# A two-block model on one core: block 2's modulation products on ScalarE and GpSimd instead of VectorE

## Chip, cores and metric

One Trainium2 chip, one NeuronCore of it. The metric is the device time of one execution in microseconds (us); a lower number is better.

## The reference, cut to what matters

Two transformer-like blocks are applied to `x` of shape 1 x 256 x 2048 (256 tokens, 2048 channels), all in float32. Each block derives six vectors of 2048 numbers from a conditioning vector `c` and uses them to shift, scale and gate the channels:

```python
c_act = jax.nn.silu(c_2)
ada = (c_act @ w_ada + b_ada)[:, None, :]        # w_ada: 2048 x 12288
sh1, sc1, gt1, sh2, sc2, gt2 = jnp.split(ada, 6, axis=-1)
h = _rms(x, g_norm1) * (1 + sc1) + sh1
...
x = x + gt1 * (merged @ w_out)
h2 = _rms(x, g_norm2) * (1 + sc2) + sh2
gate, up = jnp.split(h2 @ w_ffn_in, 2, axis=-1)
x = x + gt2 * ((jax.nn.silu(gate) * up) @ w_ffn_out)
```

That is block 2; block 1 has a recurrent mixer instead of attention and modulates in the same way. The change touches `c_act @ w_ada` of block 2: a product of a vector with a matrix of 2048 x 12288, 100.7 MB of weights that are read once.

## The kernel before

The tokens' activations stay on the chip (`xT`, channels on the 128 partitions). All weights stream from memory once, in loads of 128 x 2048 float32 (1 MB) into tiles called `raw`. Four `raw` tiles rotate (`rawp`), a fifth (`rawx`) joins during the two feed-forward parts; every load, of whatever weight, takes the next tile in turn, and all loads are issued in one fixed order on the SyncE queue.

**Matrix products.** A weight in `raw` is split into a high half `H` (ScalarE, line 333) and a low half `L` (VectorE, line 334: `raw` minus `H`, both read from SBUF), in pieces of 128 x 1024, four tiles of each. TensorE multiplies with both (lines 412 and 414 in the wide form): one load of weights is two pieces, and 16 pairs of matmuls. At the end of a strip of 512 outputs the PSUM tiles are taken over by a ScalarE copy and a VectorE add (`take`, lines 444 and 445), or added to `xT` by VectorE (line 747).

**Modulation products.** `gemv` (line 209) computes 1024 of the outputs of `c_act @ w_ada` without TensorE's matmuls: each load of `w_ada` holds two rows-of-128 by 1024 columns, and for each of the two, VectorE multiplies by the channel's silu(c) (a column of `cact`, one number per partition) and adds into the accumulator `acc` in one instruction (line 230; the first of the 16 products only multiplies, line 228). At the end TensorE transposes `acc` in eight pieces of 128 x 128 (line 241), VectorE sums over the partitions' former axis (line 242) and adds the bias (line 243). There are two accumulators (`accp`).

In block 2 this is done twelve times (six vectors, two halves): 12 x 16 = 192 products of 128 x 1024, of which 180 add and 12 only multiply. `Background` mixes them into the matrix products: after each load of a matrix product it runs as many steps as are due, and one step is one `w_ada` load with its two products. Three groups are started: `ada_a` (SC1, SH1, GT1; 6 x 16 = 96 products, one step per load, line 903) while the second half of block 1's feed-forward part runs; `ada_b` (SC2, SH2; 64 products, a step every 1.8 loads, line 1246) during attention; `ada_c` (GT2; 32 products, a step every 3 loads, line 1343) in block 2's feed-forward part. In the trace `ada_a` fills the stretch from 754 to 1089 us, called stage A below; `ada_b` the one from some 1370 to 1735 us, stage B; and `ada_c` one that ends at 2060 us.

The tile framework's scheduler then fixes the order of each engine's instructions when the program is built. Each engine runs its own list in order; semaphores make it wait.

Of the kernel before, what the change touches and what calls it, by code (L numbers as in the profile page):

```python
# [11 lines left out]
AF = mybir.ActivationFunctionType  # L12
ALU = mybir.AluOpType
# [67 lines left out]
def kernel(ctx: ExitStack, tc: tile.TileContext, a: dict, out: bass.AP):  # L81
    nc = tc.nc
    V, S, TE = nc.vector, nc.scalar, nc.tensor
# [13 lines left out]
    def ax_tile():  # L97
        return pax.tile([P, 512], F32, tag="ax", name="ax")
# [97 lines left out]
    def raw_tile(whole_only=False):  # L196
        if whole_only and spare:
            pool_, tag = spare[0]
            spare.append(spare.pop(0))
            return pool_.tile([P, 2048], F32, tag=tag, name="raw")  # L200
        turn_[0] = (turn_[0] + 1) % (4 + len(extra))
        if turn_[0] >= 4:
            pool_, tag = extra[turn_[0] - 4]
            return pool_.tile([P, 2048], F32, tag=tag, name="raw")
        return rawp.tile([P, 2048], F32, tag="raw", name="raw")
# [3 lines left out]
    def gemv(blk, parts, k0=0, nk=8):  # L209

        w = a["w_ada_2" if blk else "w_ada"][0]
        width = nk * P
        per = 2048 // width
        accs = [accp.tile([P, 1024], F32, tag="acc", name="acc") for _ in parts]
        for kt in range(0, KD, per):
            raws = []
            for part in parts:
                raw = raw_tile()
                rv = raw[:, :per * width].rearrange("p (k n) -> p k n", n=width)
                c0 = part * D + k0 * P  # L220
                nc.sync.dma_start(out=rv, in_=w[kt * P:(kt + per) * P, c0:c0 + width].rearrange("(k p) n -> p k n", p=P))
                raws.append(rv)
            for k in range(per):
                cc = cact[:, blk, kt + k:kt + k + 1]
                for acc, rv in zip(accs, raws):
                    av = acc[:, :width]
                    if kt + k == 0:
                        V.tensor_scalar(av, rv[:, k, :], cc, None, ALU.mult)
                    else:
                        V.scalar_tensor_tensor(av, rv[:, k, :], cc, av, ALU.mult, ALU.add)  # L230
                if len(parts) == 2 and k == per // 2 - 1:
                    yield
            yield
        for part, acc in zip(parts, accs):
            b = col["b_ada_2" if blk else "b_ada"][:, part * KD + k0:part * KD + k0 + nk]
            red = tiny.tile([P, nk], F32, tag=f"red{nk}", name="red")
            for q in range(0, nk, 4):
                n = min(4, nk - q)
                pt = ax_tile()
                for j in range(n):  # L240
                    TE.transpose(pt[:, j * P:(j + 1) * P], acc[:, (q + j) * P:(q + j + 1) * P], ident)  # L241
                V.tensor_reduce(red[:, q:q + n], pt[:, :n * P].rearrange("p (j t) -> p j t", t=P), AX.X, ALU.add)
            V.tensor_tensor(mods[:, blk, part, k0:k0 + nk], red, b, ALU.add)
            made.update((blk, part, k) for k in range(k0, k0 + nk))
            yield

    def whole(blk, part):
        return chain(gemv(blk, (part,), 0), gemv(blk, (part,), 8))
# [410 lines left out]
    def ada_group(i_sc, i_sh, k0, nk, paired=False):  # L659
        return gemv(0, (i_sc, i_sh), k0, nk) if paired else chain(gemv(0, (i_sc,), k0, nk), gemv(0, (i_sh,), k0, nk))  # L660
# [238 lines left out]
    def phase(half):  # L899
        if half == 0:  # L900
            bg.add(chain(*[gemv(0, (GT2,), k, 4) for k in range(0, KD, 4)]), 1.0, f"mods0{GT2}")
        else:
            bg.add(chain(whole(1, SC1), whole(1, SH1), whole(1, GT1)), 1.0, "ada_a")
# [492 lines left out]
```

## Time and profile before

| | us |
|---|---|
| median of 3 runs | 2543.78 |
| lowest, highest run | 2538.77, 2544.87 |
| the profiled execution, its own time | 2539.71 |
| its span, first to last instruction | 2538.0 |

| engine | busy us | share of the span |
|---|---|---|
| TensorE (PE), matmuls | 2451.8 | 97% |
| VectorE (DVE) | 1907.2 | 75% |
| ScalarE (ACT) | 1175.9 | 46% |
| GpSimd (POOL) | 12.1 | 0% |
| DMA, mean over the span | | 71% |

The profile comes from one execution and names its instructions by engine, line and tile: `L<-raw,H` is an instruction that writes `L` from `raw` and `H`. A group's row gives how often it ran, how long all of it was busy and one on average, and how long its engine had stood idle before it and for whom. PEld is TensorE's loading of weights into the array, and overlaps with PE. SPq is SyncE's queue, which issues the loads.

### The profile page before, as it was taken

The numbers are of one execution on the slowest core, as the hardware profiler recorded it, in microseconds if no ns is written. First come the engines' busy times: TensorE is split into PE (matmuls) and PEld (weight loads), VectorE is DVE, ScalarE is ACT, GpSimd is POOL, SyncE is SP. The second block draws the span as 40 slices with busy tenths as digits, with TensorE's granted clock in tenths as the row PEclk, the third lists the DMA queues.
The fourth block names the chain that finished last, engine by engine and source line by source line (L and its number), as shares of the span: only waits on it lengthen the run. The fifth ranks groups of instructions, "written<-read, shape, count | busy, mean of one in ns | idle before, by whom it ended". The sixth has DMA issues, their size and how long they took to land.

```text
span 2538.0 us, 36716 instructions
## 1 busy us (share of the span) xinstructions
PE 2451.8 (97%) x14677; PEld 2170.6 (86%) x14677; DVE 1907.2 (75%) x2593; ACT 1175.9 (46%) x1620; POOL 12.1 (0%) x87
## 2 busy tenths in 40 slices
PE   4989989999999999999999999999999999999999
PEld 3678989999888888888888888888788888888888
DVE  7789978977988989968757678796866665555554
ACT  2146235345334444446655447744544443444443
POOL 1000000000000000000000000000000000000000
PEclk7999989999999999999999999999999999999999
DMA  9988978966989998846547776676576765555552
GB/s 332 360 297 293 357 256 297 331 201 223 324 309 328 336 351 314 315 141 196 181 132 259 275 279 232 232 271 243 193 247 232 251 221 183 187 195 183 187 196 99
DMA packets 287548, 637.05 MB, mean 251 GB/s; under 512 B 13328, under 2 KB 18832, under 8 KB 287120
## 3 DMA queue, kind: packets, MB, share of 16 engines
q1 hardware_dynamic: 287376, 634.69, 71.4%
q8 instruction: 115, 1.88, 0.3%
q14 instruction: 57, 0.47, 0.1%
HBM read 632.56 MB, written 2.10 MB: 250 GB/s over the span
## 4 chain that ended last, share of the span: by engine, by line
PE 90%; DVE 6%; ACT 2%; DMA 2%; issue 1%; SPq 0%; ACTq 0%; DVEq 0%
PE mm L412 42%; PE mm L414 22%; PE mm L425 5%; PE mm L423 4%; PE mm L424 4%; PE mm L420 3%; DVE acc L230 2%; PE mm L477 2%; PE mm L478 2%; PE mm L476 2%; DVE L L334 1%; PE ax L241 1%; ACT H L333 1%; DMA raw<-in_w_out_dram 1%; PE mm L466 1%
## 5 line engine op out<-in xcount | busy, mean ns | idle before, releaser
L334 DVE TENSOR_TENSOR L<-raw,H 128x1024 fp32r<-128x1024 f32 (+2 forms) x816 | 954.0, 1178 | 416.2 <-ACT H L333 408.5
L333 ACT ACTIVATE H<-raw 128x1024 fp32r<-128x1024 f32 (+2 forms) x816 | 828.4, 1023 | 902.9 <-PE mm L412 631.5
L412 PE MATMUL mm<-hH,H 128*128 128x512 f32 x1536 | 546.6, 396 | 2.0 <-DVE hH L345 1.7
L412 PE MATMUL mm<-hL,H 128*128 128x512 f32 x1536 | 544.6, 395 | 0.0
L230 DVE SCALAR_TENSOR_TENSOR acc<-raw,cact,acc 128x1024 f32<-128x1024 f32 (+2 forms) x450 | 479.8, 1068 | 26.9 <-DMA raw<-in_w_ada_dram 20.8
L412 PE MATMUL mm<-fhl,H 128*128 128x512 f32 x1408 | 494.7, 395 | 0.6 <-ACT H L333 0.5
L414 PE MATMUL mm<-hH,L 128*128 128x256 f32 x1536 | 433.8, 283 | 2.1 <-DVE L L334 2.0
L414 PE MATMUL mm<-hL,L 128*128 128x256 f32 x1536 | 433.3, 283 | 0.0
L414 PE MATMUL mm<-fhl,L 128*128 128x256 f32 x1408 | 395.3, 284 | 4.6 <-DVE L L334 4.4
L412 PEld LDWEIGHTS mm<-hH,H 128*128 128x128 f32 x1536 | 289.3, 189 | 70.8 <-issue 3.7
L412 PEld LDWEIGHTS mm<-hL,H 128*128 128x128 f32 x1536 | 288.2, 188 | 66.8 <-issue 1.3
L412 PEld LDWEIGHTS mm<-fhl,H 128*128 128x128 f32 x1408 | 264.3, 188 | 61.0 <-ACT H L333 1.2
L414 PEld LDWEIGHTS mm<-hH,L 128*128 128x128 f32 x1536 | 289.5, 189 | 3.3 <-DVE L L334 2.9
L414 PEld LDWEIGHTS mm<-hL,L 128*128 128x128 f32 x1536 | 288.8, 188 | 0.5
L414 PEld LDWEIGHTS mm<-fhl,L 128*128 128x128 f32 x1408 | 264.3, 189 | 6.9 <-DVE L L334 6.4
L423 PE MATMUL mm<-hH,H 128*128 128x256 f32 x512 | 146.0, 286 | 4.9 <-ACT H L333 3.3
L425 PE MATMUL mm<-hH,L 128*128 128x256 f32 x512 | 145.7, 285 | 0.8 <-DVE L L334 0.8
L424 PE MATMUL mm<-hH,H 128*128 128x256 f32 x512 | 145.5, 284 | 0.0
L423 PE MATMUL mm<-hL,H 128*128 128x256 f32 x512 | 144.1, 282 | 0.8 <-ACT H L333 0.8
L425 PE MATMUL mm<-hL,L 128*128 128x256 f32 x512 | 143.9, 282 | 0.4 <-DVE L L334 0.3
L424 PE MATMUL mm<-hL,H 128*128 128x256 f32 x512 | 143.9, 281 | 0.0
L423 PEld LDWEIGHTS mm<-hH,H 128*128 128x128 f32 x512 | 98.0, 192 | 5.9 <-ACT H L333 3.5
(353 smaller groups left out, 2709.1 us busy)
## 6 DMA issues: line engine op xcount, KB each, us to landing
raw<-in_w_ada_dram SPq DMA_DIRECT2D x168, 1024.0 KB, 6.4
raw<-in_w_ffn_in_dram SPq DMA_DIRECT2D x88, 1024.0 KB, 4.8
raw<-in_w_in_dram SPq DMA_DIRECT2D x84, 1024.0 KB, 5.2
raw<-in_w_ffn_down_dram SPq DMA_DIRECT2D x44, 1024.0 KB, 7.2
raw<-in_w_ffn_out_dram SPq DMA_DIRECT2D x44, 1024.0 KB, 5.1
raw<-in_w_out_dram SPq DMA_DIRECT2D x32, 1024.0 KB, 6.3
raw<-in_w_ffn_gate_dram SPq DMA_DIRECT2D x26, 1024.0 KB, 7.1
raw<-in_w_ffn_up_dram SPq DMA_DIRECT2D x26, 1024.0 KB, 6.8
```

The costliest lines, as they stand in the source:

```text
L230: V.scalar_tensor_tensor(av, rv[:, k, :], cc, av, ALU.mult, ALU.add)
L333: S.activation(dh, src, AF.Copy)
L334: V.tensor_tensor(dl, src, dh.bitcast(F32), ALU.subtract)
L412: TE.matmul(o, wh[:, sl], both.rearrange("p i t -> p (i t)"), start=i == 0, stop=False, skip_group_check=True)
L414: TE.matmul(o[:, 0:T], wl[:, sl], both[:, 0, :], start=False, stop=i == n_k - 1, skip_group_check=True)
L420: TE.matmul(o, wh[:, sl], act(k0 + k), start=first, stop=last, skip_group_check=True)
L423: TE.matmul(o, wh[:, sl], both[:, 0, :], start=first, stop=False, skip_group_check=True)
L424: TE.matmul(o, wh[:, sl], both[:, 1, :], start=False, stop=False, skip_group_check=True)
L425: TE.matmul(o, wl[:, sl], both[:, 0, :], start=False, stop=last, skip_group_check=True)
L476: TE.matmul(o, xh[:, ts], wh[:, cs], start=first, stop=False)
L477: TE.matmul(o, xh[:, ts], wl[:, cs], start=False, stop=False)
L478: TE.matmul(o, xl[:, ts], wh[:, cs], start=False, stop=last)
```

## The change

For block 2 (`blk` is 1) each product becomes two instructions: ScalarE multiplies the piece of `raw` by silu(c) in place, and GpSimd adds it into the accumulator. The first product of each accumulator is a single ScalarE instruction that writes `acc`. Block 1 keeps the old form.

```diff
@@ -224,7 +224,12 @@
                 cc = cact[:, blk, kt + k:kt + k + 1]
                 for acc, rv in zip(accs, raws):
                     av = acc[:, :width]
-                    if kt + k == 0:
+                    if blk and kt + k == 0:
+                        S.activation(av, rv[:, k, :], AF.Copy, scale=cc)
+                    elif blk:
+                        S.activation(rv[:, k, :], rv[:, k, :], AF.Copy, scale=cc)
+                        nc.gpsimd.tensor_tensor(av, av, rv[:, k, :], ALU.add)
+                    elif kt + k == 0:
                         V.tensor_scalar(av, rv[:, k, :], cc, None, ALU.mult)
                     else:
                         V.scalar_tensor_tensor(av, rv[:, k, :], cc, av, ALU.mult, ALU.add)
```

Every later line of the file stands five lower in the changed kernel: the split at 333 and 334 is at 338 and 339 there, the wide matmuls at 417 and 419, the transposes at 246.

**Stage A, VectorE before and ScalarE now.** This is the end of stage A's last strip of gate and up products and the start of its down products. On VectorE before (`f`, `fhl` are the feed-forward part's hidden values):

```order
L230 SCALAR_TENSOR_TENSOR acc<-raw,cact,acc 128x1024
L845 TENSOR_TENSOR f<-f,g 128x512
L230 SCALAR_TENSOR_TENSOR acc<-raw,cact,acc 128x1024
L334 TENSOR_TENSOR fhl<-f,fhl 128x2x256
L334 TENSOR_TENSOR L<-raw,H 128x1024 x2
L230 SCALAR_TENSOR_TENSOR acc<-raw,cact,acc 128x1024 x2
```

On ScalarE in the changed kernel, at the same place:

```order
L449 ACTIVATE f<-mm 128x256
L338 ACTIVATE fhl<-f 128x2x256
L338 ACTIVATE H<-raw 128x1024
L230 ACTIVATE raw<-raw,cact 128x1024 x2
L338 ACTIVATE fhl<-f 128x2x256
L338 ACTIVATE H<-raw 128x1024 x2
L230 ACTIVATE raw<-raw,cact 128x1024 x2
```

The pair of products per load has left VectorE's list, where it stood between the pairs of `L` splits, and its multiplications now stand between ScalarE's pairs of `H` splits. The additions are two rows of 90 on GpSimd's list, which holds little else from there on.

**Stage A, SyncE's queue.** Five loads in stage A's second strip of gate weights; `DMAHW` is the semaphore of an earlier load, the other one says whose work on the tile's former content must be over. Before:

```order
L371 DMA raw<-in_w_ffn_gate_dram 128x4x512 [waits DMAHW5_49,DVE_49]
L371 DMA raw<-in_w_ffn_gate_dram 128x4x512 [waits DMAHW4_49,DVE_49]
L221 DMA raw<-in_w_ada_dram 128x2x1024 [waits DMAHW6_49,DVE_49]
L371 DMA raw<-in_w_ffn_gate_dram 128x4x512 [waits DMAHW0_49,DVE_49]
L221 DMA raw<-in_w_ada_dram 128x2x1024 [waits DMAHW7_49,DVE_49]
```

Now:

```order
L376 DMA raw<-in_w_ffn_gate_dram 128x4x512 [waits DMAHW5_49,Pool_49]
L376 DMA raw<-in_w_ffn_gate_dram 128x4x512 [waits DMAHW4_49,DVE_49]
L221 DMA raw<-in_w_ada_dram 128x2x1024 [waits DMAHW6_49,Pool_49]
L376 DMA raw<-in_w_ffn_gate_dram 128x4x512 [waits DMAHW0_49,Pool_49]
L221 DMA raw<-in_w_ada_dram 128x2x1024 [waits DMAHW7_49,DVE_49]
```

A load into a tile that held `w_ada` weights waits for GpSimd's second addition now, and all loads behind it on the queue wait with it. The loads' order is the old one but for two places in the whole program: one `w_ada` load stands a row earlier, and one, in stage B, seven loads later.

**Stage A, TensorE, the last transposes.** `ax` is the PSUM tile that the transposes of `acc` write; the rows are those around the last end of `ada_a`, with the semaphores that each waits for. Before:

```order
L412 MATMUL mm<-fhl,H 128x512
L414 MATMUL mm<-fhl,L 128x256
L241 MATMUL ax<-ident,acc 128x128 x8
L412 MATMUL mm<-fhl,H 128x512 [waits Activation_49]
L414 MATMUL mm<-fhl,L 128x256 [waits DVE_49]
```

Now:

```order
L419 MATMUL mm<-fhl,L 128x256
L246 MATMUL ax<-ident,acc 128x128 [waits Pool_49]
L246 MATMUL ax<-ident,acc 128x128 x3
L417 MATMUL mm<-fhl,H 128x512 [waits Activation_49]
L417 MATMUL mm<-fhl,H 128x512 x3
L246 MATMUL ax<-ident,acc 128x128 x2
L419 MATMUL mm<-fhl,L 128x256 [waits DVE_49]
```

The transposes wait for GpSimd now, and the first of them stands 32 matmuls earlier in TensorE's list than before. At the other eleven ends the first of them stands at its old place, and the wait is for GpSimd there too.

## Rows read from the trace of the kernel before

**Rows 1.** The page: busy time of each engine, share, instructions.

```profile
PE 2451.8 (97%) x14677; PEld 2170.6 (86%) x14677; DVE 1907.2 (75%) x2593; ACT 1175.9 (46%) x1620; POOL 12.1 (0%) x87
```

**Rows 2.** Busy time by stretch; columns as the first row names them.

```profile
core 0: us, PE busy (x) PEld busy (x) DVE busy (x) ACT busy (x) POOL busy (x), PEclk, DMA share, GB/s
754.00:1089.00 335.00, 329.77 (x1879) 287.14 (x1878) 295.10 (x327) 149.13 (x191) 0.00 (x0) 0.99 0.90 330
...
1390.00:1735.00 345.00, 341.84 (x1903) 296.45 (x1902) 279.75 (x362) 196.36 (x258) 0.00 (x0) 1.00 0.76 264
```

**Rows 3.** The same stretches, only instructions on `acc`: PE, weight loads, DVE, clock, DMA.

```profile
754.00:1089.00 335.00, 6.50 (x47) 5.55 (x48) 119.74 (x96) 0.99 0.90 330
...
1390.00:1735.00 345.00, 4.14 (x32) 3.67 (x32) 69.51 (x56) 1.00 0.76 264
```

**Rows 4.** DVE groups from 754 to 1089 us: count, busy, mean ns, idle before.

```profile
L334 DVE TENSOR_TENSOR L<-raw,H 128x1024 fp32r<-128x1024 f32 x115 | 138.2, 1220 | 18.9 <-ACT H L333 18.3
L230 DVE SCALAR_TENSOR_TENSOR acc<-raw,cact,acc 128x1024 f32<-128x1024 f32 x90 | 115.3, 1281 | 1.5 <-DMA raw<-in_w_ada_dram 0.6
...
L334 DVE TENSOR_TENSOR fhl<-f,fhl 128x512 fp32r<-128x512 f32 x10 | 6.9, 687 | 0.2
L845 DVE TENSOR_TENSOR f<-f,g 128x512 f32<-128x512 f32 x10 | 6.8, 684 | 0.0
...
L880 DVE TENSOR_TENSOR ssg<-ssg,sq 128x256 f32<-128x256 f32 x7 | 2.9, 418 | 0.0
```

**Rows 5.** What TensorE waited for, 754 to 1089 us: total us, times, longest.

```profile
PE mm L414 <- DVE L L334: 4.4, 2, 2.7
```

**Rows 6.** The same from 1089 us to the end.

```profile
PE ax L318 <- DVE diag L316: 6.5, 2, 3.6
PE mm L414 <- DVE L L334: 2.7, 2, 2.0
```

**Rows 7.** ACT groups from 754 to 1089 us.

```profile
L333 ACT ACTIVATE H<-raw 128x1024 fp32r<-128x1024 f32 x115 | 119.7, 1056 | 130.3 <-PE mm L412 92.3 <-DMA raw<-in_w_ffn_down_dram 17.5 <-PE mm L414 6.2
...
L879 ACT ACTIVATE sq<-xT,cols 128x256 f32<-128x256 f32 x7 | 3.6, 507 | 6.0 <-DVE xT L747 6.0
L879 ACT ACTIVATE sq<-xT 128x256 f32<-128x256 f32 x7 | 2.8, 401 | 0.0
```

**Rows 8.** POOL groups of the whole span.

```profile
L574 POOL TENSOR_SCALAR_AFFINE_SELECT bands<-bands 128x256 f32<-128x256 f32 x4 | 1.6, 396 | 0.0
...
L574 POOL TENSOR_SCALAR_AFFINE_SELECT bands<-bands 128x128 f32<-128x128 f32 x4 | 1.2, 290 | 0.0
```

**Rows 9.** DVE line L578: duration ns min/median/max; first and last start us.

```profile
L578 DVE TENSOR_TENSOR bands<-bands,ident x8: 278/288/375, 7.5 to 14.6; 128x128 f32<-128x128 f32 x8
```

**Rows 10.** Timeline around 7.5 us, POOL and DVE: start us, us, instruction.

```profile
7.36 0.40 POOL L576 TENSOR_SCALAR_AFFINE_SELECT bands<-bands 128x256 f32<-128x256 f32 x1
...
7.52 0.38 DVE L578 TENSOR_TENSOR bands<-bands,ident 128x128 f32<-128x128 f32 x1
...
7.71 0.34 POOL L576 TENSOR_SCALAR_AFFINE_SELECT bands<-bands 128x128 f32<-128x128 f32 x1
```

**Rows 11.** Timeline of two ends: last two products, then transposes.

```profile
1019.30 2.60 DVE L230 SCALAR_TENSOR_TENSOR acc<-raw,cact,acc 128x1024 f32<-128x1024 f32 x2
...
1024.74 0.49 PE L241 MATMUL ax<-ident,acc 128*128 128x128 f32 x3
...
1076.32 2.60 DVE L230 SCALAR_TENSOR_TENSOR acc<-raw,cact,acc 128x1024 f32<-128x1024 f32 x2
...
1088.33 1.04 PE L241 MATMUL ax<-ident,acc 128*128 128x128 f32 x8
```

**Rows 12.** What load issues on SP waited for, 754 to 1089 us.

```profile
SPq L371 <- DVE acc L230: 63.4, 28, 4.9
...
SPq L221 <- DVE acc L230: 31.2, 14, 6.4
```

**Rows 13.** Busy time of VectorE line L334 alone by stretch.

```profile
1390.00:1735.00 345.00, 147.05 (x127) 1.00 0.76 264
```

## The prediction

> **What bounds the kernel now.** The page's first part comes first: TensorE is busy for 97% of the span, VectorE for 75%, ScalarE for 46%, and GpSimd has next to nothing to do [rows 1]. A share over the whole span says little about one stage, so the next view is busy time by stretch [rows 2]. The work of the change lies in three stretches; the same view for instructions on `acc` alone counts the products: 96 of the 192 run in stage A, within 335 us, and 56 of the other 96 within the 345 us of stage B [rows 3]. Stage A is where things are dense: TensorE 329.8 of 335 us, VectorE 295.1 (88%), ScalarE 149.1 (45%), transfers 90% [rows 2]. VectorE does two kinds of work there in about equal parts, 115 `L` splits (138 us) and 96 products (120 us) [rows 3, 4]. That looks like an engine worth relieving. But the question is what TensorE waits for, and the view of its waits answers: in stage A, 4.4 us in all for VectorE's `L` [rows 5]; after it to the end, 2.7 us for `L`, and 6.5 us in the norms' short chains, where no product is queued [rows 6]. So the kernel is bound by TensorE. VectorE, at 88%, is the next in line and almost never late.
>
> **The change part by part.** The sum starts at the profiled execution's own 2539.7 us; the median of the three runs, 2543.8, lies 4.1 above, and I add that at the end. About 0.3% (7.6 us) is the least that a measurement of this kernel can tell from no change.
>
> *What leaves VectorE:* 180 multiply-adds of 1.281 us and 12 multiplications of some 0.75 us, 240 us in all, of which 120 in stage A [rows 3, 4]. The gain is bounded by what TensorE waits for behind them: nothing at the least, 4.4 + 2.7 = 7.1 us at the most [rows 5, 6]. I take 2.7, the part outside stage A, because inside stage A the last term below takes VectorE's new room away again.
>
> *What ScalarE gets:* 192 multiplications. A 128x1024 copy takes 1.056 us; a scale read from a column costs 0.106 us more (the same square with and without it: 0.507 and 0.401) [rows 7]. That is 1.16 us each, 223 us in all, and 96 x 1.16 = 111 us in stage A, where ScalarE goes from 149 to 260 of 335 us (78%). The cover is its idle time: in stage A it stood 92 us before its splits because TensorE had not yet freed an `H` tile [rows 7]. A multiplication can stand before a PSUM take-over or a split for 1.16 us, as a product of 1.28 us stood before VectorE's half of the same work. I cost it at nothing. Without that cover, each of stage A's 13 strip ends could lose 1.16 us, 15 us in all.
>
> *What GpSimd gets:* 180 additions of 128x1024 with both inputs in SBUF, 90 in stage A. The trace has no such row. GpSimd's nearest ones read one input: 128x128 in 0.290 us and 128x256 in 0.396 [rows 8], so 0.83 ns per element and 0.18 us fixed. That gives three prices: 1.03 us if the second input costs nothing, 1.88 if each input costs what the one does, 2.73 if the write costs as much again. I take 1.88, since the row's one price already holds a write. Stage A's additions then take 90 x 1.88 = 169 us, half of the stage. In a pure count GpSimd keeps up easily.
>
> *What the additions wait for, and who waits for them.* Before, the two products of a load ended 2.6 us after their start; now it is 1.16 + 2 x 1.88 = 4.9 us, 2.4 later. Behind it are two waits. First, the `raw` tile is freed later: 28 loads of matrix weights in stage A had their issue held by a product, 63.4 us together, and 14 `w_ada` loads, 31.2 us [rows 12]; each is now 2.4 us later. The `H` and `L` tiles, split two loads ahead, cover that: ScalarE waited more for TensorE (92.3 us) than for the down weights' transfers (17.5) [rows 7]. If that cover went, 28 x 2.4 = 67 us would show. Second, the transposes of `acc` in TensorE's list wait for the last addition. The last product ended at 1019.30 + 2.60 = 1021.9 and the transposes began at 1024.74; at the last end 1078.9 and 1088.33, where they now stand 32 matmuls earlier, 32 x 335/1879 = 5.7 us, so the room of 9.4 shrinks to 3.7 [rows 2, 11]. Both hold 2.4 us. I cost them at nothing.
>
> *What the two engines cost each other.* This is the term that decides. In the first microseconds VectorE runs eight equal subtractions of two SBUF inputs, beside GpSimd's mask building. Their median is 0.288 us, the longest 0.375 [rows 9], and a long one, at 7.52, lies beside a GpSimd instruction that reads SBUF; the GpSimd instruction next to it took 0.34 us where 0.290 is usual [rows 8, 10]. So VectorE with two SBUF inputs and a reading GpSimd slow each other down, both of them. The Trainium skill (SBUF — State Buffer, "Who interferes with whom") says that such a pair shares an exclusive lock and that the later one fully blocks until the other is done; the row above agrees with its sign, and by the rule the sum is the one that I take, while by the row's 0.09 us alone nothing would be lost. If they take turns, their times add up. VectorE's instructions with two SBUF inputs in stage A are the splits (138.2 + 6.9), `f` times `g` (6.8) and the two sums of squares (2 x 2.9), 157.7 us [rows 4]; with GpSimd's 169 that is 327 of 335 us. Two in-order engines do not fill a stage to 98%: the fullest one behind TensorE filled 88% of it. At that filling 327 us need 327 / 0.881 = 371 us, 36 more than the stage has, and TensorE waits for `L` in that time. In stage B, 60 additions take 113 us beside 147 us of splits [rows 13], 260 / 0.881 = 295 of 345 us: nothing there, nor in the last stretch.
>
> The sum is 2539.7 - 2.7 + 36 = 2573 us, and with the 4.1 us to the median **2577 us**, slower by 1.3%. The Trainium skill (GPSIMD Engine Reference, section 3.1) gives 4497 ns for an addition of 2048 elements, from which I estimate 2.25 us here; the same sum would be 2616 us by that.
>
> **The rivals.**
>
> *Hidden.* The turn-taking costs only some 0.09 us per VectorE instruction whatever its size, as the one row shows. 115 x 0.09 = 10 us of VectorE's time vanish in the 160 us that it has spare once the products are gone. For it: TensorE's waits are tiny now. Against it: 0.09 us is most of what a 128-element instruction spends on its data, so nothing says that it stays 0.09 at 1024. Time 2544 (2540 to 2550).
>
> *Faster.* VectorE's room shows: the `L` splits in the down products of stage A no longer queue behind products, and all of TensorE's waits for `L` go, 7.1 us, with 0.5 us or so of small ones around them. It decides in this direction only if a split beside an addition loses less than its share of the room, some 1 us. Time 2536. Against it: it needs nearly every wait to go, and none to come.
>
> *Heavier.* An addition costs more than 1.88 us; halfway to the upper price, 2.3, stage A needs (207 + 158) / 0.881 = 414 us, 79 more: 2620. At 2.73 it would be 458 and 2664. For it: nothing in the trace shows a two-input instruction on GpSimd.
>
> *The transposes.* GpSimd falls behind by two loads, 4 x 1.88 = 7.5 us, and TensorE stands at the ends of `ada_a` before transposes whose last addition is 7.5 + 2.4 = 9.9 us late against rooms of 2.8 and 3.7 us [rows 11]: 7.1 + 6.2 = 13 us, 2557. Here the place of the loss is another, and its size is less.
>
> That the change does not do what it says can be set aside: the order of the instructions shows 180 additions on GpSimd and none of block 2's products on VectorE.
>
> **How the numbers follow.** Forecast 0.40, heavier 0.22, transposes 0.06, hidden 0.24, faster 0.08. The forecast, the heavier case and the transposes are slower: 0.68. Hidden is within 0.3%: 0.24. Faster: 0.08. The range goes from 2538, which leaves out the faster case, to 2640, which takes in the heavier case but for the upper third of it: 0.08 + 0.07 are left out. The likeliest case's own range is 2560 to 2595.
>
> **What would show it.** GpSimd's additions at 1.9 us or more, longer where a split runs beside them, and `L` splits well over 1.22 us in stage A; TensorE waiting for `L` (or for transposes) by tens of us there; the stretch from `ada_a`'s first product to its last transposes near 371 us instead of 335; later stretches unchanged. I am wrong if the splits keep 1.22 us beside the additions, or if the splits grow and TensorE still does not wait, since the tiles split ahead would then have covered it.

## The result, and where the time went

The change makes the kernel slower: 2688.85 us (median of 4 runs, 2682.48 to 2692.03) against 2543.37 before, a ratio of 1.0572 with a 95% interval of 1.0548 to 1.0596. That is 145 us, where 33 were forecast and 2640 us was the upper end of the range. The sign was right, and so was the mechanism for the first of the stages; that the later stages would lose nothing was wrong.

The first part of the page of the changed kernel, the profiled execution (span 2687.0 us, against 2538.0), in answer to [rows 1]:

```profile
PE 2509.2 (93%) x14677; PEld 2203.1 (82%) x14677; DVE 1961.8 (73%) x2401; ACT 1363.0 (51%) x1811; POOL 525.5 (20%) x267
```

The 192 instructions that VectorE lost held 240 us, and it is still busy for 55 us more than before: what is left on it takes longer. TensorE issues the same 14677 matmuls, is busy for 57 us longer and idle for 177.8 us instead of 86.2, 92 more; 57 and 92 are the 149 us between the two spans.

Busy time by stretch, columns as in [rows 2]. The stretches are cut at the same work as before (the same count of matmuls, within 1%): stage A (`ada_a`), what lies between, stage B (`ada_b`), the rest to the last transposes (called stage C here, `ada_c`), and the tail.

```profile
761.00:1149.00 388.00, 350.87 (x1887) 298.84 (x1887) 334.14 (x230) 245.28 (x288) 269.70 (x90) 0.95 0.79 285
1149.00:1463.00 314.00, 298.77 (x1664) 257.51 (x1663) 213.44 (x420) 179.00 (x333) 26.12 (x41) 0.98 0.49 162
1463.00:1864.00 401.00, 365.49 (x1907) 310.24 (x1906) 291.76 (x308) 248.20 (x311) 138.53 (x52) 0.95 0.66 231
1864.00:2210.00 346.00, 325.84 (x1806) 282.84 (x1806) 234.75 (x255) 185.47 (x237) 80.21 (x29) 0.97 0.60 213
2210.00:2687.00 477.00, 472.73 (x2704) 414.15 (x2702) 257.80 (x292) 201.57 (x233) 0.00 (x0) 1.00 0.52 177
```

Stage A takes 388 us where the forecast said 371. But stage B takes 401 instead of 345, with VectorE at 73% and GpSimd at 35%. To see how much is lost where, I counted TensorE's matmuls in stretches of 20 us in each trace and read off when the same share of them was through. This is how far a kernel is behind the one before, in us, at five points of before's time, good to some 5 us (the labels of the experiments are explained below):

| at before's | 754 | 1089 | 1390 | 1735 | 2060 |
|---|---|---|---|---|---|
| the change | 10 | 60 | 73 | 130 | 151 |
| only `ada_a` (e6) | 9 | 60 | 61 | 60 | 59 |
| only `ada_b`, `ada_c` (e7) | 5 | 4 | 12 | 70 | 90 |
| GpSimd only writes (e3) | 8 | 2 | 2 | 3 | 0 |
| two copies (e12) | 7 | 26 | 31 | 61 | 64 |
| more VectorE time (e8) | 7 | 70 | 71 | 93 | 93 |
| longer splits, evenly (e14) | 7 | 10 | 11 | 13 | 13 |

The 5 to 10 us at 754 lie ahead of the first product of block 2; e3, which ends level, has them too, so they are no part of the change's loss. Stage A loses 50 us, and all that follows to the last transposes 90 more; nothing is lost after them.

**The turns.** VectorE's groups of stage A (columns as in [rows 4]), by which `L` has gone from 1.220 to 2.335 us and `f` times `g` from 0.684 to 1.860, while the take-overs from PSUM, which read one SBUF input, keep their 0.42 us:

```profile
L339 DVE TENSOR_TENSOR L<-raw,H 128x1024 fp32r<-128x1024 f32 x114 | 262.0, 2335 | 30.9 <-ACT H L338 30.1 <-PE mm L417 0.8
L850 DVE TENSOR_TENSOR f<-f,g 128x512 f32<-128x512 f32 x10 | 18.6, 1860 | 0.1
...
L450 DVE TENSOR_TENSOR f<-mm,f 128x256 f32<-128x256 f32 x20 | 8.2, 418 | 6.7 <-ACT f L449 6.6
```

The additions' own line (duration in ns, shortest, median, longest; first and last start) and, from the timeline, one stretch of GpSimd and what VectorE did beside it (start, us):

```profile
L231 POOL TENSOR_TENSOR acc<-acc,raw x180: 2341/2810/3462, 765.6 to 2196.7; 128x1024 f32<-128x1024 f32 x180
```

```profile
784.04 19.62 POOL L231 TENSOR_TENSOR acc<-acc,raw 128x1024 f32<-128x1024 f32 x6 [6.26 <-ACT raw L230]
```

```profile
789.01 9.04 DVE L339 TENSOR_TENSOR L<-raw,H 128x1024 fp32r<-128x1024 f32 x3 [1.01 <-ACT H L338]
```

An undisturbed addition takes 2.34 us. Six in a row take 3.27 each beside three splits of 3.01 each, and the longest addition, 3.46 us, is an undisturbed one and 1.12 more, about one split. The two engines do take turns, a whole instruction at a time.

**What TensorE waits for** (total us, times, longest), in the first four stretches of the table, one after the other; before, `L` made 4.4 and 2.7 [rows 5, 6]:

```profile
PE mm L419 <- DVE L L339: 18.7, 16, 2.9
PE mm L417 <- DVE g L450: 7.4, 6, 1.8
PE mm L417 <- DVE f L450: 3.4, 2, 1.8
PE ax L246 <- POOL acc L231: 2.9, 2, 2.7
...
PE mm L417 <- DVE xT L752: 2.1, 2, 1.8
...
PE mm L417 <- DVE qs_t L450: 8.8, 2, 6.7
...
PE mm L419 <- DVE L L339: 1.1, 3, 0.7
...
PE mm L417 <- DVE jn L457: 9.0, 6, 3.4
PE mm L417 <- DVE B L450: 7.0, 3, 6.0
...
PE mm L482 <- DVE L L339: 4.0, 5, 1.7
...
PE mm L419 <- DVE L L339: 2.7, 5, 1.0
PE mm L417 <- DVE ks_t L450: 2.4, 1, 2.4
PE mm L417 <- DVE xT L752: 2.2, 3, 0.8
...
PE mm L417 <- DVE f L450: 6.2, 2, 4.8
PE mm L417 <- DVE g L450: 5.0, 4, 3.5
```

The rows of `L` make 26.5 us. The rows of L450, L457 and L752 make 53.5 us: they are the take-overs of finished sums from PSUM (`f`, `g`, `qs_t`, `ks_t`, `jn`, `B` and `xT` are the tiles that they write), which do not take turns themselves, and TensorE's next matmuls wait for them.

What makes them late differs by stage. In stage A nearly all of TensorE's waits of over 1 us, followed back from each instruction to what released it, come to splits and other two-input instructions of VectorE that were held up: a take-over stands behind them in VectorE's list. Behind stage A the longest waits come another way. Here is the longest, 6.74 us, with the rows of TensorE, VectorE, ScalarE, GpSimd and SyncE's queue that lead to it:

```profile
1460.41 0.79 PE L417 MATMUL mm<-hH,H 128*128 128x512 f32 x1 [6.74 <-DVE qs_t L450]
...
1458.47 1.54 DVE L339 TENSOR_TENSOR L<-raw,H 128x1024 fp32r<-128x1024 f32 x1 [9.03 <-ACT H L338]
...
1455.31 2.19 ACT L230 ACTIVATE raw<-raw,cact 128x1024 f32<-128x1024 f32 x2 [10.27 <-DMA raw<-in_w_ada_dram]
...
1440.34 5.75 POOL L231 TENSOR_TENSOR acc<-acc,raw 128x1024 f32<-128x1024 f32 x2 [9.45 <-ACT raw L230]
1456.59 5.67 POOL L231 TENSOR_TENSOR acc<-acc,raw 128x1024 f32<-128x1024 f32 x2 [10.49 <-ACT raw L230]
...
1446.58 0.46 SPq L221 DMA_DIRECT2D raw<-in_w_ada_dram  x1
```

Two additions end at 1446.09 us; only then is their `raw` tile free, the queue goes on with a load that waited for it, and behind that one it issues this `w_ada` load, at 1446.58. ScalarE stands for 10.27 us before the multiplication that needs it, with the split and the take-over copy behind it in its list; VectorE stands for 9.03 us for that split, and TensorE for the take-over. GpSimd has nothing to do for 10.49 us, until 1456.59: for most of this time nobody takes turns with anybody. Behind stage A there are 23 waits of over 1 us, 60 us together; twelve of them, 35 us, lead back to a multiplication on ScalarE whose load had not landed, and most of the others to VectorE's stretched instructions or to the norms' chains that wait before as well.

**The clock.** TensorE's mean granted clock is 0.95 to 0.98 in the four stretches and 1.00 in the tail, where no addition runs; before it was 0.99 in stage A and 1.00 in stage B [rows 2]. Two neighbouring stretches around stage B's beginning, same columns, with VectorE's turns in both:

```profile
1400.00:1450.00 50.00, 46.84 (x263) 40.09 (x262) 26.83 (x24) 26.83 (x31) 17.00 (x6) 1.00 0.59 205
1450.00:1500.00 50.00, 39.56 (x200) 33.51 (x199) 26.08 (x20) 24.41 (x30) 21.83 (x8) 0.90 0.58 215
```

Where TensorE stood idle for 10 us of 50, the mean is 0.90, which at the two levels of 1.2 and 2.4 GHz is a fifth of the time at the lower. So an idle gap is paid for a second time, in slower matmuls. Of the 57 us by which TensorE is busy longer I put some 42 down to the clock: that is an estimate, by weighting the busy time of each microsecond of both traces with the clock granted in it.

### The profile page after: what moved, and what is told of

Same layout as the page of the kernel before. It is cut to its first block, busy times and chain, and to the rows that moved or that the text cites. A ratio compares the mean times of both kernels' runs of the same rounds, so it can differ in the third digit from the quotient of the medians.

```text
span 2687.0 us, 37112 instructions
## 1 busy us (share of the span) xinstructions
PE 2509.2 (93%) x14677; PEld 2203.1 (82%) x14677; DVE 1961.8 (73%) x2401; ACT 1363.0 (51%) x1811; POOL 525.5 (20%) x267
## 3 DMA queue, kind: packets, MB, share of 16 engines
q8 instruction: 115, 1.88, 0.3%
## 5 line engine op out<-in xcount | busy, mean ns | idle before, releaser
L339 DVE TENSOR_TENSOR L<-raw,H 128x1024 fp32r<-128x1024 f32 (+2 forms) x816 | 1164.4, 1444 | 478.2 <-ACT H L338 471.0
L231 POOL TENSOR_TENSOR acc<-acc,raw 128x1024 f32<-128x1024 f32 x180 | 513.4, 2852 | 1630.5 <-ACT raw L230 1590.8
L417 PE MATMUL mm<-hH,H 128*128 128x512 f32 x1536 | 566.3, 406 | 46.7 <-DVE g L450 12.4
L417 PE MATMUL mm<-hL,H 128*128 128x512 f32 x1536 | 552.9, 399 | 3.0 <-DVE hL L350 3.0
L419 PE MATMUL mm<-hH,L 128*128 128x256 f32 x1536 | 441.2, 288 | 0.9 <-DVE L L339 0.9
L417 PEld LDWEIGHTS mm<-hH,H 128*128 128x128 f32 x1536 | 297.3, 194 | 125.3 <-DVE g L450 15.6
L419 PEld LDWEIGHTS mm<-hH,L 128*128 128x128 f32 x1536 | 298.3, 194 | 1.8 <-DVE L L339 1.5
L230 ACT ACTIVATE raw<-raw,cact 128x1024 f32<-128x1024 f32 x180 | 201.3, 1141 | 123.1 <-DMA raw<-in_w_ada_dram 121.7
L235 DVE SCALAR_TENSOR_TENSOR acc<-raw,cact,acc 128x512 f32<-128x512 f32 (+2 forms) x270 | 249.7, 928 | 16.8 <-DMA raw<-in_w_ada_dram 12.6
L430 PE MATMUL mm<-hH,L 128*128 128x256 f32 x512 | 145.8, 285 | 0.8 <-DVE L L339 0.8
L428 PE MATMUL mm<-hL,H 128*128 128x256 f32 x512 | 144.3, 282 | 0.7 <-ACT H L338 0.7
```

Source lines behind the costliest of these rows:

```text
L230: S.activation(rv[:, k, :], rv[:, k, :], AF.Copy, scale=cc)
L231: nc.gpsimd.tensor_tensor(av, av, rv[:, k, :], ALU.add)
L339: V.tensor_tensor(dl, src, dh.bitcast(F32), ALU.subtract)
L417: TE.matmul(o, wh[:, sl], both.rearrange("p i t -> p (i t)"), start=i == 0, stop=False, skip_group_check=True)
L419: TE.matmul(o[:, 0:T], wl[:, sl], both[:, 0, :], start=False, stop=i == n_k - 1, skip_group_check=True)
L428: TE.matmul(o, wh[:, sl], both[:, 0, :], start=first, stop=False, skip_group_check=True)
```

## The experiments

Each edit is to lines 230 and 231 of the changed kernel unless another place is shown.

### Which engine: e1 to e4

```diff
# e1_act_dve
-    nc.gpsimd.tensor_tensor(av, av, rv[:, k, :], ALU.add)
+    V.tensor_tensor(av, av, rv[:, k, :], ALU.add)
# e2_dve_pool
-    S.activation(rv[:, k, :], rv[:, k, :], AF.Copy, scale=cc)
+    V.tensor_scalar(rv[:, k, :], rv[:, k, :], cc, None, ALU.mult)
# e3_pool_writes
-    nc.gpsimd.tensor_tensor(av, av, rv[:, k, :], ALU.add)
+    nc.gpsimd.memset(rv[:, k, :], 0.0)
+    nc.gpsimd.memset(rv[:, k, :], 0.0)
+    nc.gpsimd.memset(av, 0.0)
# e4_act_only
-    nc.gpsimd.tensor_tensor(av, av, rv[:, k, :], ALU.add)
```

> The change without GpSimd: ScalarE multiplies by silu(c) in place, VectorE adds (180 additions of two SBUF inputs, about 1.2 us each, in the place of the 1.28 us products). If the lost time comes from VectorE and GpSimd taking turns, it is all gone: 2540 to 2552 us, L splits back to 1.22 us in the first dense stretch, TensorE idle near 86 us. If it comes from the multiplication in ScalarE's in-order list (123 us of waiting for w_ada loads, take-overs queued behind), it stays: 2670 to 2700 us, and TensorE still waits for the take-overs f, g, jn, B.

2552.16 us, ratio 1.0033 (1.0020 to 1.0046): the loss is gone but for 0.3%, and ScalarE still makes all the multiplications. The group of the additions in stage A, now on VectorE:

```profile
L231 DVE TENSOR_TENSOR acc<-acc,raw 128x1024 f32<-128x1024 f32 x90 | 109.8, 1220 | 6.1 <-ACT raw L230 3.4
```

> The change without ScalarE: VectorE multiplies in place (about 0.73 us each, one input), GpSimd adds. If the two engines' turn-taking is the cause, it stays: 2680 us or more (VectorE has 0.73 us x 180 = 131 us more to do than in the change), L splits at 2.2 us, additions at 2.8 us. If ScalarE's list is the cause, the time returns to 2540 to 2560 us.

2761.49 us, ratio 1.0847 (1.0831 to 1.0864): without ScalarE's part it is worse. VectorE's multiplication, with one SBUF input, takes turns as well; its line (ns) shows 734 undisturbed and 2902 at most:

```profile
L230 DVE TENSOR_SCALAR raw<-raw,cact x180: 734/747/2902, 758.3 to 2260.5; 128x1024 f32<-128x1024 f32 x180
```

> GpSimd is as long busy as in the change and frees raw and acc as late, but reads nothing: after ScalarE's multiplication it writes zeros twice into raw and once into acc (3 x 0.95 = 2.85 us, the mean of an addition in the change). Left out: the sum into acc. If turn-taking over reads is the cause: 2540 to 2560 us and L splits at 1.22 us. If the late release of raw and acc, or the wait of ScalarE for the loads, is the cause: 2660 to 2700 us with L splits at 1.22 us.

2540.14 us, ratio 0.9971 (0.9958 to 0.9985). GpSimd is busy for 514.9 us, 525.5 in the change, and nothing is lost. The lines (ns) of `L` and of the first of the three writes, and one row of its timeline:

```profile
L341 DVE TENSOR_TENSOR L<-raw,H x816: 679/1224/1228, 156.7 to 2522.1; 128x1024 fp32r<-128x1024 f32 x149, 128x512 fp32r<-128x512 f32 x10, 128x576 fp32r<-128x576 f32 x3, 128x768 fp32r<-128x768 f32 x2
...
L231 POOL MEMSET raw<- x180: 942/954/971, 764.2 to 2041.2; 128x1024 f32 x180
```

```profile
776.21 5.00 POOL L233 MEMSET acc<- 128x1024 f32 x5
```

No split takes longer than before, and no write longer than another. The release of `raw` is not as late as was expected: the writes to `acc` need no `raw` and run ahead, as in the row, so that GpSimd is done with a piece of `raw` 3.0 us after the end of its multiplication on the mean, against 4.3 in the change. So the loss takes GpSimd's reading, or the last 1.3 us of the hold. e12 below speaks against the hold alone: there it is 4.6 us, and 55 us are lost instead of 145.

> ScalarE's multiplications alone, nothing on GpSimd or VectorE for the 180 additions. Left out: the sum into acc. Turn-taking as the cause: 2533 to 2545 us, the most that relieving VectorE can bring. ScalarE's in-order list as the cause: 2640 us or more, with 100 us or more of ScalarE waiting for w_ada loads and TensorE waiting for take-overs.

2542.62 us, ratio 0.9987 (0.9977 to 0.9996). This is the bound on what the change could have brought: with the additions left out altogether 0.13% is won. ScalarE's wait for `w_ada` loads, 121.7 us in the change, is 21.9 here (26.5 in e3), so that wait comes with the reading additions; the multiplications alone do not make it.

### Which stage: e6 and e7

The parts 0 to 2 are `ada_a`'s, 3 to 5 those of `ada_b` and `ada_c`; e7 has `parts[0] > 2` in both places.

```diff
# e6_only_a
-    if blk and kt + k == 0:
+    if blk and parts[0] <= 2 and kt + k == 0:
...
-    elif blk:
+    elif blk and parts[0] <= 2:
```

> Only the 96 products of ada_a on the new path, the other 96 on VectorE as before. The trace of the change puts some 50 to 60 us of its loss into that stage: if the losses of the stages stand by themselves, 2595 to 2610 us. If all comes from the dense stage, as forecast, and the later loss is only its echo: 2670 us or more.

2597.98 us, ratio 1.0211 (1.0190 to 1.0232): 52 us.

> Only the 96 products of ada_b and ada_c on the new path, ada_a on VectorE as before. If every stage with additions loses by itself, whatever VectorE's share of busy time there: 2620 to 2640 us, 80 to 90 over before. If stages with room on VectorE lose nothing, as forecast: 2540 to 2555 us.

2631.19 us, ratio 1.0338 (1.0318 to 1.0358): 85 us. The two add up to 136 of the 145 us, and the table above shows each loss in its own stages. The greater part is lost where VectorE and GpSimd both have room.

### How long a hold: e5, e10, e12

```diff
# e5_halves
-    nc.gpsimd.tensor_tensor(av, av, rv[:, k, :], ALU.add)
+    for h in range(0, width, 512):
+        nc.gpsimd.tensor_tensor(av[:, h:h + 512], av[:, h:h + 512], rv[:, k, h:h + 512], ALU.add)
# e10_pool_copy; e12_two_copies has the new line twice
-    nc.gpsimd.tensor_tensor(av, av, rv[:, k, :], ALU.add)
+    nc.gpsimd.tensor_copy(av, rv[:, k, :])
```

> The change with each addition as two of 512 columns (some 1.25 us each instead of 2.34 alone), so that VectorE can be let in between; the sum held is the same or a little more. If the total time that GpSimd holds the shared port sets the loss: 2685 to 2710 us, as the change or worse. If the length of a single hold sets it (a split or a take-over late by up to 2.34 us): half of the loss goes, 2600 to 2650 us, and the longest L split of 1024 columns falls from 3.4 to about 2.5 us.

2707.95 us, ratio 1.0637 (1.0614 to 1.0661): the first case, worse than the change. The lines (ns) of `L` and of the half additions:

```profile
L340 DVE TENSOR_TENSOR L<-raw,H x816: 683/1225/2391, 151.8 to 2685.9; 128x1024 fp32r<-128x1024 f32 x149, 128x512 fp32r<-128x512 f32 x10, 128x576 fp32r<-128x576 f32 x3, 128x768 fp32r<-128x768 f32 x2
...
L232 POOL TENSOR_TENSOR acc<-acc,raw x360: 1256/1732/2375, 757.8 to 2213.0; 128x512 f32<-128x512 f32 x180
```

The longest split fell to 2.39 us as expected, and it did not help: 360 halves take 628.7 us, 0.49 more each than undisturbed, so turns cost a product 0.98 us, where they cost a whole addition 2.85 - 2.34 = 0.51 (513.4 us for 180).

> GpSimd copies raw over acc instead of adding: one input from SBUF, some 1.03 us by the price of its one-input rows, instead of 2.34. Left out: the sum. If every GpSimd instruction that reads SBUF takes the port for its whole length, the loss is less in proportion to the hold or better: 2555 to 2615 us, the copies and the 1024-column splits both up to 2.25 us long at most. If only a two-input addition collides: 2535 to 2548 us, with splits at 1.22 us.

2545.51 us, ratio 1.0003 (0.9993 to 1.0012). Neither case as a whole: the time is the second's, the long splits are the first's. The copy does take turns, and it costs nothing. The lines (ns) of `L` and of the copy:

```profile
L339 DVE TENSOR_TENSOR L<-raw,H x816: 682/1225/2065, 157.1 to 2530.9; 128x1024 fp32r<-128x1024 f32 x149, 128x512 fp32r<-128x512 f32 x10, 128x576 fp32r<-128x576 f32 x3, 128x768 fp32r<-128x768 f32 x2
...
L231 POOL COPY acc<-raw x180: 1037/1044/2102, 765.5 to 2050.8; 128x1024 f32<-128x1024 f32 x180
```

> Two copies of raw over acc in GpSimd in the place of one addition: 2 x 1.04 = 2.08 us of reading for each product, where one copy (1.04 us) lost nothing and the addition (2.34 us) loses 145 us. Left out: the sum. If the length of the hold for each product is what counts, whatever the operation: 2600 to 2670 us, L splits of the first dense stretch at 1.8 to 2.2 us. If it is the two-input addition: 2543 to 2555 us as with one copy.

2599.35 us, ratio 1.0214 (1.0197 to 1.0231): just under the first case's range, with `L` at 1.72 us in the first dense stretch. A one-input read costs too, once it is long enough. By undisturbed hold for each product, 1.04 us loses nothing, 2.08 us 55, 2.34 us 145 and 2 x 1.26 = 2.51 us 162. The loss does not grow in proportion. Nor is the length of a single hold what counts: one copy of 1.04 us loses nothing and two of the same length lose 55. From 2.08 to 2.34 us the operation changes too, so no run shows what the length alone does there.

### What the later stages lose: e8, e9, e11, e13, e14, e15

```diff
# e8_dve_load: e1, and behind it
+    V.scalar_tensor_tensor(rv[:, k, :], rv[:, k, :], cc, rv[:, k, :], ALU.mult, ALU.add)
# e9_add_only
-    S.activation(rv[:, k, :], rv[:, k, :], AF.Copy, scale=cc)
# e14_long_splits: e3, and in weights(), behind split(...)
+    live = {t["name"] for t in bg.tasks if t["live"]}
+    again = 768 if "ada_a" in live else 512 if live & {"ada_b", "ada_c"} else 0
+    if again and n * width == 1024:
+        c = again // n
+        V.tensor_tensor(wl[:, :, :c], rv[:, k:k + n, :c], wh[:, :, :c].bitcast(F32), ALU.subtract)
```

> No GpSimd: ScalarE multiplies, VectorE adds (1.22 us), and then VectorE does one more multiply-add of 1.28 us on raw, whose result nobody reads: 230 us more of VectorE's time, as much as its splits and sums of two SBUF inputs grew in the change, and raw freed as late. VectorE is then busy for about 2120 us, against 1962 in the change. If VectorE's lost time as such makes the loss: 2690 us or more. If it is where the waits fall (unplanned, in front of splits and take-overs): 2555 to 2620 us.

2631.07 us, ratio 1.0330 (1.0304 to 1.0356), between the two cases. VectorE is busy for 2091 us, 130 more than in the change, and yet the loss is 85 us, 63 of them in stage A, where VectorE is at 95%. Before's stage A in this run, columns as in [rows 2]:

```profile
754.00:1089.00 335.00, 301.59 (x1611) 254.71 (x1610) 319.75 (x328) 208.79 (x238) 0.00 (x0) 0.93 0.77 273
```

In the stages behind it only 23 are lost. So a full VectorE can cost a stage like A as much as the change does, but it does not explain the 90 us of the later ones.

> As the run in which GpSimd only writes (no turn-taking, 2540 us), but VectorE computes a part of each 1024-column L a second time while block 2's modulation products run: 768 columns in the first dense stretch (1.22 + 0.95 = 2.2 us for each L, 2.3 in the change) and 512 later (1.22 + 0.69 = 1.9 us, 1.6 in the change). Left out: the sum into acc. If longer splits by themselves make the loss, of the dense stretch and of the later ones: 2630 to 2700 us. If it needs the uneven turns (a split or a take-over held for up to 3.4 us): 2540 to 2575 us. If only the dense stretch is sensitive to VectorE's time: 2575 to 2610 us, all the loss before 1150 us.

2551.98 us, ratio 1.0030 (1.0017 to 1.0044). GpSimd is about as long busy as in the change (515.5 us), and VectorE's time for an `L` is near what it was there, 2.17 us in stage A and about 1.9 later (2.34 and 1.58 there), but nothing takes turns. Stage A, columns as in [rows 2]:

```profile
754.00:1089.00 335.00, 328.56 (x1862) 284.07 (x1861) 274.26 (x339) 243.41 (x285) 249.09 (x270) 0.99 0.86 318
```

The splits' length and GpSimd's, on the mean, cost 7 us. Two things of the change are missing here: the turns, which make single splits and additions late unevenly, and the late release of `raw` (2.8 us after the multiplication on the mean, 4.3 in the change). This run does not tell one from the other.

> The change without ScalarE's 180 multiplications: GpSimd adds raw as it was loaded. Left out: the factor silu(c) of all but the first product of each vector. The additions hold the port as before, but nothing stands in ScalarE's list to wait for a w_ada load; GpSimd alone waits for it. If ScalarE's blocked list is what carries the loss of the later stages: the 90 us there shrink to 30 or less, 2600 to 2635 us in all. If the turn-taking of VectorE and GpSimd carries it by itself: 2670 us or more.

2660.73 us, ratio 1.0453 (1.0434 to 1.0472), below the second case and far above the first. ScalarE's multiplications, and its waits for the loads in front of them, carry some 30 of the 145 us; with them gone ScalarE waits for weights in front of `H` instead, 52.9 us for `in_w_in` alone. The traced execution of e9 took 2675.49 us, 15 over the median; in it the stages behind A lose some 62 us instead of 90, and stage A 65 instead of 50. So one link of the chain shown for the 6.74 us wait is broken here, and the late loads reach TensorE by another way.

Three runs told less. e11 writes each `w_ada` load one step ahead of its products (the loop's other lines read `kk` and `use` in the places of `kt` and `raws`):

```diff
-        for kt in range(0, KD, per):
+        last = None
+        for kt in range(0, KD + per * blk, per):
...
-            for part in parts:
+            for part in parts if kt < KD else ():
...
-            for k in range(per):
+            last, now = (kt, raws), last if blk else (kt, raws)
+            for k in range(per if now else 0):
+                kk, use = now
```

> The change with each w_ada load written one step of the list ahead of its products (one step more for each vector). ScalarE should not find its load still on the way. If its wait for the loads (123 us) carries the loss of the later stages: 2600 to 2645 us, with that wait under 40 us. If the turn-taking carries it, the wait of ScalarE goes and the loss stays: 2670 us or more.

2674.95 us, ratio 1.0506 (1.0488 to 1.0525). The time is the second case's, but ScalarE's wait for the loads did not go (119.8 us), so it does not test what it was made for. e13 makes GpSimd read one column of `raw` and then add `acc` to itself:

```diff
-    nc.gpsimd.tensor_tensor(av, av, rv[:, k, :], ALU.add)
+    nc.gpsimd.tensor_copy(gate, rv[:, k, :1])
+    nc.gpsimd.tensor_tensor(av, av, av, ALU.add)
```

> GpSimd reads one column of raw, which frees it, and then adds acc to itself: the same hold of 2.34 us at the same place, but raw is free again before the addition and not after it. Left out: the products' sum (acc is doubled instead). If raw tiles freed late, and loads issued late for it, carry the loss of the later stages: it falls there from 80 or 90 us to under 40, 2600 to 2645 us in all. If it is VectorE's splits and take-overs that stand in the port's queue: 2665 us or more.

2739.29 us, ratio 1.0766 (1.0748 to 1.0784), but it did not free `raw` early: the one-column reads stood in GpSimd's list behind additions, and single load issues waited for them for up to 23.6 us. It is inconclusive. e15 gives the ring a fifth `raw` tile from the end of the stick-breaking part to the end of `ada_b`:

```diff
     att.close()
+    more = ExitStack()
+    xr = more.enter_context(tc.tile_pool(name="xr", bufs=1))
+    extra[:] = [(xr, f"rx{i}") for i in range(1)]
...
-    att_slots.close()
     bg.finish("ada_b")
+    extra.clear()
+    more.close()
+    att_slots.close()
```

> The change with a fifth raw tile from the end of the stick-breaking part to the end of ada_b (from about 1740 to 1862 us in the trace of the change, where some 20 us are lost). If loads held up by raw tiles that come free late carry the loss, it falls there to under 10 us: 2665 to 2680 us. If it is VectorE's late splits and take-overs: 2683 to 2695 us.

2687.11 us, ratio 1.0550 (1.0522 to 1.0578). Nothing is gained, the second case. What TensorE waited for from 1745 to 1866 us, of the change first and of e15 second:

```profile
PE mm L417 <- DVE jn L457: 6.8, 4, 3.4
```

```profile
PE mm L417 <- DVE jn L457: 10.0, 4, 6.1
```

There the take-overs are what TensorE waits for, with four tiles and with five. This does not hold for the whole of the later stages: the longest waits there, shown above, go back to late loads.

No version that does the same work beats the kernel before. The two that come out below it, by 0.29% (e3) and 0.13% (e4), leave out the sum.

## Why the prediction went wrong

- **Taking turns**: right. The Trainium skill (SBUF — State Buffer, "Who interferes with whom") says that a VectorE instruction with two SBUF inputs and a reading GpSimd exclude each other in full, and that a GpSimd instruction that only writes does not contend. The trace agrees with both: splits of 1.22 us last up to 3.44, and beside 515 us of writes (e3) none is over 1.228. The 0.09 us of [rows 9] can be the small end of the same thing, since both instructions there were short, and the *hidden* rival that took it for the price falls.
- **"I take 1.88"** for an addition: too low. 2.34 us undisturbed lies within the bounds of 1.03 and 2.73, next to the *heavier* rival's 2.3, whose 2620 us is still 69 us short. The Trainium skill's figure (GPSIMD Engine Reference, section 3.1), 2.25 us by the estimate, was nearer than the 1.88 worked out from rows.
- **Stage A, "two in-order engines do not fill a stage to 98%"**: the mechanism held, since the turns need more time than the stage had, but the number was near by two errors that offset each other. With the true price the sum is 157.7 + 90 x 2.34 = 368 us, which at the 0.881 used would give 418; the stage took 388, filled to 95%. By the matmuls it lost 50 us instead of 36.
- **"Nothing there, nor in the last stretch"**: the step that failed. It judged stage B by whether the turns fit into its 345 us. They do, even at 2.34 us (60 x 2.34 + 147 = 287 us; the 60 are all of `ada_b`'s additions, of whose 64 products 56 lie in the 345 us [rows 3]), and the later stages still lost 90 of the 145 us, as e7 shows by itself with 85.
- **"I cost them at nothing"**, of the late release of `raw`, and "I cost it at nothing", of ScalarE's multiplications: wrong together in the later stages. Each is cheap without reading additions beside it (e1, e4, and e3 for a release after 3.0 us). With them, a `w_ada` load is issued late, ScalarE's list stands at the multiplication that needs it (121.7 us in all), and over half of TensorE's long waits behind stage A, 35 of 60 us, come from there. e9, without the multiplications, loses some 30 us less. For the transposes the cost of next to nothing was right (2.9 us in stage A).
- **What is queued behind**: the take-overs from PSUM were not in the sum at all. They keep their 0.42 us, and TensorE waits more for them (53.5 us) than for `L` (26.5).
- **The clock** had no term: by the estimate above, 42 us of longer matmuls.
- **The gain**, bounded by 7.1 us: by the medians e3 won 6 us and e4 3, so the bound held.

What stays open is how the 90 us of the later stages divide between the two ways: held-up instructions in VectorE's list, and late loads at which ScalarE's list stands. The trace of the change shows both, e9 gives some 30 us to one link of the second, and the run that was to free `raw` early (e13) did not do so. Nor was it shown why an addition costs so much more than two copies of nearly its length.

## What to carry to other kernels

Before elementwise work that reads SBUF goes to GpSimd, look in the same stretch for VectorE's two-input instructions and for what stands behind them in its list (here take-overs from PSUM, which pay for turns that they take no part in), and follow the tile that GpSimd holds: which load waits for it, and which engine's list stands before that load (here ScalarE's). That the sum of the busy times fits into a stage does not settle it. And leaving the moved work out altogether (e4) tells for one run's price what moving it can bring at best, here 0.13%.

## What was not expected of the hardware

- An addition of 128x1024 with two SBUF inputs takes GpSimd 2.34 us undisturbed, VectorE 1.22 (e1).
- GpSimd's one-input copy (1.037 us undisturbed) takes turns with VectorE's splits as well: `L` up to 2.065 us, the copy up to 2.102 (e10).
- VectorE's multiplication by a column, with one SBUF input, takes turns too: 0.734 us undisturbed, up to 2.902 beside the additions (e2). The same page of the Trainium skill (SBUF — State Buffer, "Who interferes with whom") counts `tensor_scalar` among those that can take the shared pair, and the trace agrees.
- Shorter pieces made it worse, not better: two halves of an addition lose more to turns than the whole one, 0.98 us against 0.51 (e5).
